# Turning the probability-times-value product of one attention block around: values as the stationary operand

## The chip, the cores and the metric

The kernel runs on one core of a Trainium2 chip. The metric is the time of one execution in microseconds (us) of device time. Of the core's engines, PE (TensorE) multiplies matrices (its loads of stationary operands are listed apart, as PEld), DVE (VectorE) and ACT (ScalarE) do elementwise work and read what PE leaves in PSUM, POOL (GpSimd) does elementwise work in SBUF alone, and SP (SyncE) issues most DMA transfers.

## What is computed

Two transformer blocks over 256 tokens of width 1024, all in 32-bit floating point. The first has sixteen attention heads of width 64 (eight "fox" heads with a forget gate, eight "moba" heads with a relative bias), then a mixture of 32 experts; the second has a Fourier branch, a differential attention and two dense feed-forward layers. Only the attention of the first block is touched. For each head, cut from the reference:

```
s = einsum('bhqd,bhkd->bhqk', q, k) * scale      # plus gate or bias terms, causal mask
p = softmax(s, axis=-1)
y = einsum('bhqk,bhkd->bhqd', p, v)
...
mix = concatenate([y_a, y_b], axis=-1)           # 16 heads x 64 = 1024 features
x = x + gt_m * rms_norm(mix @ w_out, g_post_mix)
```

## The kernel before

Queries are cut into two tiles of 128. The causal mask leaves the first tile 128 keys and the second 256, so the probabilities of a head are one tile `s` of 128 x 384. A head h goes through these helpers:

- `scores(h)`: PE writes q k^T into a PSUM tile of the name `sc` (two buffers, shared with several other steps).
- `soft(h)`: for each query tile DVE adds bias and mask and finds the largest score (L671), ACT takes the exponential and its row sums (L673); at the end DVE inverts both sums (L675, tile `sm`). `s` stays undivided.
- `trans(h)`: three PE transposes of `s` into the PSUM tile `pt` (L684); ACT (odd heads, and all from 8 on) or DVE copies it to the SBUF tile `st`.
- `pv(h)`: three matmuls (L701, L702, L704) with a 128 x 128 piece of `st` as the stationary operand and 64 columns of v as the moving one. Queries come out on partitions, a pair of heads beside each other in the one PSUM tile `mix`. DVE then multiplies each query tile by its inverse sum into an SBUF tile `mix` (L707).
- `mixT(j)`: two PE transposes of head pair j (L713) put features on partitions, in a tile `sc`; ACT rounds it to the high part `mh` (L714), DVE subtracts for the low part `ml` (L715; both are `big_h` and `big_l` in the trace). They are the stationary operands of the output projection.

The order of all engines' work is the order in which the code is written: step by step over h, and every engine takes its instructions in that order. Steps 0 to 7 (fox) are mixed with projections for the moba heads. In steps 8 to 16 the helper `out_products(n)` puts n units of the output projection (three matmuls of 512 columns each) between `scores` and `pv`, and `Stream` splits the next weight piece into high part (ACT, L250) and low part (DVE, L251). Steps 8 to 11 also hold a long DVE reduction for the modulation vector, `ada_cols` (L375). The core of a step from 8 on:

```
trans(h - 1); scores(h); soft(h)
...
out_products({8: 2, 9: 2, 11: 2, 13: 2, 16: 2}.get(h, 4))
j = {9: 3, 11: 4, 13: 5, 15: 6}.get(h)
if j:
    mixT(j)
...
pv(h - 1)
```

Pairs 0 and 1 are turned in step 7, pair 2 in step 8, pair 7 after the last step. Behind the attention stand the residual, the second norm, the router and the experts, whose weights come through a ring of 2 MB buffers; further buffers of it open when the attention's are given back.

Of the kernel before, what the change touches and what calls it, by code (L numbers as in the profile page):

```python
# [21 lines left out]
F32 = mybir.dt.float32  # L22
# [4 lines left out]
AF = mybir.ActivationFunctionType  # L27
OP = mybir.AluOpType
# [4 lines left out]
T, D, KD = 256, 1024, 8  # L33
# [62 lines left out]
def build(tc, A, out, dbg=None):  # L96
    nc = tc.nc
# [28 lines left out]
    ident, ones, iota, sel3 = c1[:, 0:128], c1[:, 128:256], c1[:, 256:384], c1[:, 384:416]  # L126
# [513 lines left out]
    PT = {}  # L640

    def head(h):
        return ("a", h) if h < 8 else ("b", h - 8)
# [19 lines left out]
    def soft(h):  # L663
        p = PT[h]
        n, hd = head(h)
        s = pa.tile([128, 384], F32, name="s", bufs=2)
        nm = pa.tile([128, 2], F32, name="nm", bufs=2)
        sm = pa.tile([128, 2], F32, name="sm", bufs=4)
        b = mask if n == "a" else biasM[:, hd]
        for i, (c0, c1_, b0) in enumerate(((0, 128, 128), (128, 384, 0))):  # L670
            nc.vector.tensor_tensor_reduce(out=s[:, c0:c1_], in0=p[:, i, 0:c1_ - c0], in1=b[:, b0:256], scale=-1.0,  # L671
                                           scalar=3.0e38, op0=OP.add, op1=OP.min, accum_out=nm[:, i:i + 1])
            nc.scalar.activation(s[:, c0:c1_], s[:, c0:c1_], AF.Exp, bias=nm[:, i:i + 1], scale=-1.0,  # L673
                                 accum_out=sm[:, i:i + 1])
        nc.vector.reciprocal(sm, sm)  # L675
        PT[h] = (s, sm)

    pmix, st_ = {}, {}

    def trans(h):  # L680
        s, _ = PT[h]
        pt = ps.tile([128, 384], F32, name="pt", bufs=1)
        for i in range(3):
            nc.tensor.transpose(pt[:, 128 * i:128 * i + 128], s[:, 128 * i:128 * i + 128], ident)  # L684
        st_[h] = pa.tile([128, 384], F32, name="st", bufs=2)
        if h % 2 or h > 7:
            nc.scalar.activation(st_[h], pt, AF.Copy)
        else:
            nc.vector.tensor_copy(st_[h], pt)

    def pv(h):
        n, hd = head(h)
        _, sm = PT.pop(h)
        st = st_.pop(h)
        if h % 2 == 0:
            pmix[h // 2] = (ps.tile([128, 2, 128], F32, name="mix", bufs=1),
                            pa.tile([128, 2, 128], F32, name="mix", bufs=4))
        pm_, mx = pmix[h // 2]
        o = slice(64 * (h % 2), 64 * (h % 2) + 64)
        v = vt[n][:, :, 64 * hd:64 * hd + 64]  # L700
        nc.tensor.matmul(pm_[:, 0, o], lhsT=st[:, 0:128], rhs=v[:, 0], start=True, stop=True, skip_group_check=True)  # L701
        nc.tensor.matmul(pm_[:, 1, o], lhsT=st[:, 128:256], rhs=v[:, 0], start=True, stop=False,  # L702
                         skip_group_check=True)
        nc.tensor.matmul(pm_[:, 1, o], lhsT=st[:, 256:384], rhs=v[:, 1], start=False, stop=True,  # L704
                         skip_group_check=True)
        for i in range(2):
            nc.vector.tensor_scalar(mx[:, i, o], pm_[:, i, o], sm[:, i:i + 1], None, op0=OP.mult)  # L707

    def mixT(j, tag="sc", bufs=2):
        _, mx = pmix.pop(j)  # L710
        pt = ps.tile([128, T], F32, name=tag, bufs=bufs)
        for i in range(2):
            nc.tensor.transpose(pt[:, 128 * i:128 * i + 128], mx[:, i], ident)  # L713
        nc.scalar.activation(mh[:, j], pt, AF.Copy)  # L714
        nc.vector.tensor_tensor(ml[:, j], pt, mh[:, j].bitcast(F32), op=OP.subtract)  # L715


    proj_out("b")
    for h in range(8):
# [5 lines left out]
        if h > 1:  # L725
            soft(h)
# [4 lines left out]
        j = {1: 4, 3: 5, 4: 6, 6: 7}.get(h)  # L731
# [96 lines left out]
    for h in range(8, 17):  # L828
# [11 lines left out]
        j = {9: 3, 11: 4, 13: 5, 15: 6}.get(h)  # L840
# [15 lines left out]
        if h == 14:  # L856

            lgc = pa.tile([128, NE], F32, name="lgc")
            p = ps.tile([128, NE], F32, name="sc", bufs=2)
            for k in range(KD):  # L860
                nc.tensor.matmul(p, lhsT=mod[:, 24 + k:25 + k].to_broadcast([128, 128]), rhs=wr[:, k], start=(k == 0),
                                 stop=(k == KD - 1))
            nc.vector.tensor_add(lgc, p, V("b_router"))
        if h == 15:
# [196 lines left out]
    for i in range(4):  # L1061
        nc.tensor.matmul(pm[:, i], lhsT=rows[i // 2][:, 128 * (i % 2):128 * (i % 2) + 128], rhs=sel4[:, 0:2], start=True,
                         stop=True, skip_group_check=True)

    p = ps.tile([128, 4, 128], F32, name="pt", bufs=1)
    for tt in range(2):
        for k in range(KD):
            nc.tensor.matmul(p[:, k % 4, 64 * (k // 4):64 * (k // 4) + 64], lhsT=h2t[:, tt, 128 * k:128 * k + 128],
                             rhs=S0[:, tt], start=(tt + k == 0), stop=(tt == 1), skip_group_check=True)
# [12 lines left out]
    ps = fm.enter_context(tc.tile_pool(name="pse", bufs=1, space=PSUM, reuse_waits="tile"))  # L1082
# [359 lines left out]
    for e in range(NE):  # L1442
# [5 lines left out]
        if e == NE - 1:  # L1448
# [7 lines left out]
        v = nc.values_load(cnt[0:1, e:e + 1], engines=[ET.PE, ET.Activation, ET.DVE], min_val=0, max_val=T,  # L1456
                           skip_runtime_bounds_check_because="a count of at most 256 tokens")
# [77 lines left out]
    for k in range(KD):  # L1535
        nc.tensor.matmul(acc[k], lhsT=pend[0][:, 128 * k:128 * k + 128], rhs=pend[1], start=False, stop=True,
                         skip_group_check=True)
# [516 lines left out]
```

## Time and profile before

| what | value |
|---|---|
| time, median of 3 runs | 1770.94 us (1769.97 to 1772.21) |
| time of the profiled execution | 1769.94 us |
| span in its trace | 1768.1 us |
| PE busy | 1501.6 us, 85% of the span |
| PE weight loads | 984.5 us, 56% |
| DVE busy | 779.3 us, 44% |
| ACT busy | 522.3 us, 30% |
| mean granted TensorE clock | 0.949 of full |
| read from HBM | 545.25 MB, 309 GB/s over the span |

The attention of the first block lies between 75 and 190 us of the span; the experts between 214 and 1265 us; the second block fills the rest. Shares over the whole span mix these stages, so they say nothing on the change by themselves. The time is 1.8 us more than the span.

### The profile page before, as it was taken

How to read it: one execution, taken by the hardware profiler on the slowest of the kernel's cores; microseconds unless marked ns; L12 is line 12 of the kernel's file. 1: busy time of each engine (PE TensorE's matmuls, PEld its weight loads, DVE VectorE, ACT ScalarE, POOL GpSimd, SP SyncE). 2: the span in 40 equal slices, each digit the busy share in tenths (PEclk: the TensorE clock that was granted, in tenths of full speed). 3: DMA queues.
4: the chain of work that ended last, by engine and by line, in shares of the span. 5: the costliest groups of instructions: out<-in, count | busy, mean ns of one | idle time of the engine just before them, and what ended most of it. 6: DMA issues, size and time to landing. Idle time of an engine off the chain costs nothing. (4 is left out here: it accounts for less than half of the span.)

```text
span 1768.1 us, 26974 instructions
## 1 busy us (share of the span) xinstructions
PE 1501.6 (85%) x10842; PEld 984.5 (56%) x10842; DVE 779.3 (44%) x1605; ACT 522.3 (30%) x1114; POOL 106.5 (6%) x114
## 2 busy tenths in 40 slices
PE   6999978967779888778868776668999999999998
PEld 5787623323233332332323222227999989999997
DVE  5776613233332432433211111115766767676665
ACT  4544311101011010110101101005544556565444
POOL 3501100000000000000000000002000100310000
PEclk8999999998999999999979888889999999999999
DMA  9878779999999979999999999995554553344630
GB/s 353 323 229 340 277 271 414 417 415 416 416 401 412 413 290 366 415 415 417 406 383 402 409 416 416 416 414 218 191 205 159 193 201 144 143 165 170 221 137 25
DMA packets 89049, 549.49 MB, mean 311 GB/s; under 512 B 5064, under 2 KB 7912, under 8 KB 49448
## 3 DMA queue, kind: packets, MB, share of 16 engines
q1 hardware_dynamic: 88424, 544.55, 77.9%
q8 instruction: 154, 2.52, 0.6%
q0 software_dynamic: 272, 0.92, 0.2%
q10 hardware_dynamic: 144, 1.05, 0.2%
q14 instruction: 55, 0.45, 0.1%
HBM read 545.25 MB, written 1.25 MB: 309 GB/s over the span
## 5 line engine op out<-in xcount | busy, mean ns | idle before, releaser
L251 DVE TENSOR_TENSOR wl<-ring,wh 128x512 fp32r<-128x512 f32 x421 | 284.9, 710 | 114.8 <-ACT wh L250 108.1
L250 ACT ACTIVATE wh<-ring 128x512 fp32r<-128x512 f32 x424 | 248.7, 622 | 106.5 <-PE gu L281 86.1
L1259 PE MATMUL h<-ring,xe 128*32 128x512 f32 x1280 | 194.5, 733 | 56.4 <-DMA ring<-in_w_gate_up 32.4
L280 PE MATMUL gu<-ring,wh 128*128 128x256 f32 x704 | 201.2, 286 | 2.9 <-ACT ring L1586 2.9
L281 PE MATMUL gu<-ring,wh 128*128 128x256 f32 x704 | 200.4, 285 | 1.9 <-DVE ring L1590 1.9
L282 PE MATMUL gu<-ring,wl 128*128 128x256 f32 x704 | 200.4, 285 | 0.0
L1155 PE MATMUL h<-ring,xe 128*64 128x512 f32 x768 | 173.6, 594 | 11.4 <-DMA ring<-in_w_gate_up 9.8
L1259 PEld LDWEIGHTS h<-ring,xe 128*32 128x32 f32 x1280 | 50.4, 127 | 181.5 <-issue 145.8
L1264 DVE TENSOR_SCALAR glu<-h 64x512 f32<-64x512 f32 x23 | 15.7, 683 | 287.5 <-PE h L1259 287.5
L280 PEld LDWEIGHTS gu<-ring,wh 128*128 128x128 f32 x704 | 135.9, 193 | 3.5 <-ACT ring L1586 3.3
L281 PEld LDWEIGHTS gu<-ring,wh 128*128 128x128 f32 x704 | 135.9, 193 | 2.2 <-DVE ring L1590 2.1
L282 PEld LDWEIGHTS gu<-ring,wl 128*128 128x128 f32 x704 | 135.9, 193 | 0.0
L1117 ACT ACTIVATE xg<-rot 128x512 f32<-128x512 f32 x28 | 16.7, 597 | 381.4 <-PE rot L1114 381.4
L1155 PEld LDWEIGHTS h<-ring,xe 128*64 128x64 f32 x768 | 56.6, 137 | 113.1 <-issue 96.5
L280 PE MATMUL pd<-acth,wh 128*128 128x256 f32 x352 | 98.8, 281 | 0.1
L281 PE MATMUL pd<-actl,wh 128*128 128x256 f32 x352 | 98.3, 279 | 0.1
L282 PE MATMUL pd<-acth,wl 128*128 128x256 f32 x352 | 98.2, 279 | 0.0
L1286 PE MATMUL h<-ring,aT 128*32 128x256 f32 x1280 | 78.2, 394 | 21.2 <-ACT aT L1281 10.7
L1195 PE MATMUL h<-ring,aT 128*64 128x512 f32 x384 | 86.7, 605 | 6.4 <-ACT aT L1175 6.4
L1372 DVE COPY_PREDICATED bias<-bm,vecs 128x512 f32<-128x512 uint8 x124 | 80.0, 726 | 1.1
L1160 DVE TENSOR_SCALAR glu<-h 128x512 f32<-128x512 f32 x12 | 8.3, 692 | 160.6 <-PE h L1155 160.6
L280 PE MATMUL gu<-big_h,wh 128*128 128x256 f32 x256 | 74.6, 291 | 0.0
(446 smaller groups left out, 2450.2 us busy)
## 6 DMA issues: line engine op xcount, KB each, us to landing
ring<-in_w_gate_up SPq DMA_DIRECT2D x127, 2048.0 KB, 23.2
ring<-in_w_down SPq DMA_DIRECT2D x62, 2048.0 KB, 24.6
ring<-in_ffn_gu SPq DMA_DIRECT2D x22, 2048.0 KB, 8.0
ring<-in_win SPq DMA_DIRECT2D x12, 2048.0 KB, 8.2
ring<-in_ffn_wd SPq DMA_DIRECT2D x10, 2048.0 KB, 9.5
ring<-in_ada SPq DMA_DIRECT2D x8, 2048.0 KB, 11.5
ring<-in_wout SPq DMA_DIRECT2D x4, 2048.0 KB, 7.8
ring<-in_ada SPq DMA_DIRECT2D x4, 1024.0 KB, 12.4
```

The source lines that it names most:

```text
L250: nc.scalar.activation(dh, src, AF.Copy)
L251: (eng or nc.vector).tensor_tensor(dl, src, dh.bitcast(F32), op=OP.subtract)
L280: nc.tensor.matmul(o, lhsT=wh, rhs=mh, start=start, stop=False, skip_group_check=True)
L281: nc.tensor.matmul(o, lhsT=wh, rhs=ml, start=False, stop=False, skip_group_check=True)
L282: nc.tensor.matmul(o, lhsT=wl, rhs=mh, start=False, stop=stop, skip_group_check=True)
L1117: nc.scalar.activation(x, p, AF.Copy)
L1155: nc.tensor.matmul(p[64 * hf:64 * hf + 64], lhsT=x, rhs=wk[:, 512 * hf:512 * hf + 512], start=False, stop=(k == KD - 1), skip_group_check= ...
L1195: nc.tensor.matmul(py[64 * oh_:64 * oh_ + 64], lhsT=at[:, j, 64 * c:64 * c + 64], rhs=wk[:, 512 * oh_:512 * oh_ + 512], start=False, stop= ...
L1259: nc.tensor.matmul(p[32 * g:32 * g + 32], lhsT=x(k), rhs=w[:, k % 2, c], start=False, stop=(k == KD - 1), skip_group_check=True)
L1264: nc.vector.tensor_scalar(g, p[0:64], 7.0, None, op0=OP.min)
L1286: nc.tensor.matmul(py[32 * g:32 * g + 32, 0:T], lhsT=at[:, j, 32 * c:32 * c + 32], rhs=w[:, j, T * g:T * g + T], start=False, stop=(c == 1 ...
L1372: nc.vector.copy_predicated(bias2[:, h], m, val[:, :, None].to_broadcast([128, 2, T]))
```

## The change

`soft` divides: after L675, DVE multiplies both pieces of `s` by the inverse sums (new L677, 128 x 128 and 128 x 256). `pv` becomes two matmuls (new L702, L703) with 64 columns of v as the stationary operand and `st` as the moving one (256 and 128 columns), so a head's features come out on 64 partitions of a PSUM tile `mix` of 128 x 256 and a pair fills it. L707's multiplications go, and so do `mixT`'s transposes: ACT (new L711) and DVE (new L712) read the pair as it is. For pairs 0 to 2 DVE first copies it to SBUF (new L707); from pair 3 on they read the PSUM tile itself. That tile has one buffer.

```diff
         nc.vector.reciprocal(sm, sm)
-        PT[h] = (s, sm)
+        for i, c in enumerate((slice(0, 128), slice(128, 384))):
+            nc.vector.tensor_scalar(s[:, c], s[:, c], sm[:, i:i + 1], None, op0=OP.mult)
+        PT[h] = s
...
     def pv(h):
...
         if h % 2 == 0:
-            pmix[h // 2] = (ps.tile([128, 2, 128], F32, name="mix", bufs=1),
-                            pa.tile([128, 2, 128], F32, name="mix", bufs=4))
-        pm_, mx = pmix[h // 2]
+            pmix[h // 2] = ps.tile([128, T], F32, name="mix", bufs=1)
+        p = pmix[h // 2]
...
-        nc.tensor.matmul(pm_[:, 0, o], lhsT=st[:, 0:128], rhs=v[:, 0], start=True, stop=True, skip_group_check=True)
-        nc.tensor.matmul(pm_[:, 1, o], lhsT=st[:, 128:256], rhs=v[:, 0], start=True, stop=False,
+        nc.tensor.matmul(p[o], lhsT=v[:, 0], rhs=st[:, 0:256], start=True, stop=False, skip_group_check=True)
+        nc.tensor.matmul(p[o, 128:256], lhsT=v[:, 1], rhs=st[:, 256:384], start=False, stop=True,
                          skip_group_check=True)
-        nc.tensor.matmul(pm_[:, 1, o], lhsT=st[:, 256:384], rhs=v[:, 1], start=False, stop=True,
-                         skip_group_check=True)
-        for i in range(2):
-            nc.vector.tensor_scalar(mx[:, i, o], pm_[:, i, o], sm[:, i:i + 1], None, op0=OP.mult)
-
-    def mixT(j, tag="sc", bufs=2):
-        _, mx = pmix.pop(j)
-        pt = ps.tile([128, T], F32, name=tag, bufs=bufs)
-        for i in range(2):
-            nc.tensor.transpose(pt[:, 128 * i:128 * i + 128], mx[:, i], ident)
-        nc.scalar.activation(mh[:, j], pt, AF.Copy)
-        nc.vector.tensor_tensor(ml[:, j], pt, mh[:, j].bitcast(F32), op=OP.subtract)
+        if h in (1, 3, 5):
+            pmix[h // 2] = pa.tile([128, 256], F32, name="mix", bufs=4)
+            nc.vector.tensor_copy(pmix[h // 2], p)
+
+    def mixT(j):
+        p = pmix.pop(j)
+        nc.scalar.activation(mh[:, j], p, AF.Copy)
+        nc.vector.tensor_tensor(ml[:, j], p, mh[:, j].bitcast(F32), op=OP.subtract)
```

Three places in the order of instructions show what moves. On PE in step 9, with the semaphores that an instruction waits for in brackets, this is the piece from `mixT(3)` over `pv(8)` to `trans(9)` (`vb` is v of the moba heads, `c_70` the identity):

```order
-L713 MATMUL sc<-c_70,mix 128x128 [waits DVE_49] x2
-L701 MATMUL mix<-vb,st 128x64 [waits Activation_49]
-L702 MATMUL mix<-vb,st 128x64
-L704 MATMUL mix<-vb,st 128x64
-L684 MATMUL pt<-c_70,s 128x128 [waits PE_49,Activation_49]
-L684 MATMUL pt<-c_70,s 128x128 [waits Activation_49]
-L684 MATMUL pt<-c_70,s 128x128
-L659 MATMUL sc<-qkb 128x128 [waits DVE_49]
+L702 MATMUL mix<-st,vb 64x256 [waits DVE_49]
+L703 MATMUL mix<-st,vb 64x128
+L686 MATMUL pt<-c_70,s 128x128 [waits PE_49]
+L686 MATMUL pt<-c_70,s 128x128 x2
```

The first matmul of `pv(8)` waited for ACT (the copy `st`) and now waits for a count of DVE's; the wait of the next scores (L659) for DVE is gone.

On DVE in the same step, from the inverse sums of head 9 on, this stood there before (`ring` holds the modulation weights and the weight piece):

```order
L675 RECIPROCAL sm<-sm 128x2 [waits Activation_49]
L375 ISA ring_1076,mod<-ring_1076,csb 128x1024
L375 ISA mod 128x1
L251 TENSOR_TENSOR wl<-ring_941,wh 128x512 [waits Activation_49]
L715 TENSOR_TENSOR big_l<-sc,big_h 128x256 [waits Activation_49]
```

This stands there now:

```order
L675 RECIPROCAL sm<-sm 128x2 [waits Activation_49]
L677 TENSOR_SCALAR s<-s,sm 128x128 [waits DVE_49]
L677 TENSOR_SCALAR s<-s,sm 128x256
L375 ISA ring_1079,mod<-ring_1079,csb 128x1024
L375 ISA mod 128x1
L251 TENSOR_TENSOR wl<-ring_941,wh 128x512 [waits Activation_49]
L712 TENSOR_TENSOR big_l<-mix,big_h 128x256 [waits Activation_49]
```

L712 stands where L715 stood, behind the same reduction and split and two scalings more; it now reads the PSUM tile `mix` that `pv(8)` writes next.

On DVE in step 1, behind the sums of head 0, the scalings come ahead of two weight splits and the copy of the transposed head:

```order
-L251 TENSOR_TENSOR wl<-ring_284,wh 128x512 [waits DVE_49,Activation_49] x2
-L689 COPY st<-pt 128x384 [waits PE_49]
+L677 TENSOR_SCALAR s<-s,sm 128x128 [waits DVE_49]
+L677 TENSOR_SCALAR s<-s,sm 128x256
+L251 TENSOR_TENSOR wl<-ring_284,wh 128x512 [waits Activation_49] x2
+L691 COPY st<-pt 128x384 [waits PE_49]
```

The transposes of head 0 (L686) now follow these scalings, where they followed ACT's exponentials.

## Rows read from the trace of the kernel before

**Rows 1.** Stretches: busy us of PE, PEld, DVE, ACT, POOL; granted clock, DMA share, GB/s.

```profile
175.00:186.00 11.00, 11.00 (x79) 8.83 (x79) 4.93 (x16) 4.22 (x11) 0.00 (x0) 1.00 0.31 102
200.00:214.00 14.00, 13.10 (x98) 11.50 (x100) 7.96 (x38) 4.36 (x11) 1.03 (x2) 0.88 0.95 376
214.00:1265.00 1051.00, 816.78 (x5594) 350.71 (x5591) 308.32 (x640) 150.24 (x332) 25.30 (x26) 0.92 0.95 383
```

**Rows 2.** Timeline of step 9, DVE and PE: start, us, operation, idle before.

```profile
148.29 0.17 DVE L675 RECIPROCAL sm<-sm 128x2 f32<-128x2 f32 x1 [0.77 <-ACT s L673]
148.38 1.20 DVE L375 CUSTOM_DVE_ANT_0 ring<-ring,csb 128x1024 f32<-128x1024 f32 x1
149.51 0.69 DVE L251 TENSOR_TENSOR wl<-ring,wh 128x512 fp32r<-128x512 f32 x1
150.11 0.41 DVE L715 TENSOR_TENSOR big_l<-sc,big_h 128x256 fp32r<-128x256 f32 x1
...
148.27 0.38 PE L713 MATMUL sc<-c,mix 128*128 128x128 f32 x2
148.49 0.33 PE L701 MATMUL mix<-vb,st 128*128 128x64 f32 x2
...
149.11 0.49 PE L684 MATMUL pt<-c,s 128*128 128x128 f32 x3
```

**Rows 3.** Timeline of DVE in the second block's attention, which scales such a tile.

```profile
1426.91 0.17 DVE L1754 RECIPROCAL sm<-sm 128x2 f32<-128x2 f32 x1 [0.82 <-ACT s L1752]
1427.11 0.16 DVE L1755 TENSOR_TENSOR sm<-sm,nlam 128x1 f32<-128x1 f32 x1
1427.19 0.35 DVE L1756 TENSOR_SCALAR s<-s,sm 128x256 f32<-128x256 f32 x1
```

**Rows 4.** Timeline of DVE and PE around steps 7 to 9.

```profile
140.09 0.17 DVE L675 RECIPROCAL sm<-sm 128x2 f32<-128x2 f32 x1 [0.71 <-ACT s L673]
141.89 0.29 DVE L671 CUSTOM_DVE_ANT_0 s<-sc,bias 128x128 f32<-128x128 f32 x1 [0.40 <-issue]
146.88 0.29 DVE L671 CUSTOM_DVE_ANT_0 s<-sc,bias 128x128 f32<-128x128 f32 x1 [0.42 <-PE sc L659]
...
144.78 0.43 PE L701 MATMUL mix<-va,st 128*128 128x64 f32 x2
```

**Rows 5.** Timeline of steps 13 and 14, DVE and PE.

```profile
166.64 0.17 DVE L675 RECIPROCAL sm<-sm 128x2 f32<-128x2 f32 x1 [0.77 <-ACT s L673]
166.83 0.33 PE L701 MATMUL mix<-vb,st 128*128 128x64 f32 x2
169.24 0.92 PE L659 MATMUL sc<-qkb 64*128 64x128 f32 x4 [0.36 <-ACT csb L810]
```

**Rows 6.** Timeline of step 15, DVE and PE.

```profile
179.04 0.17 DVE L675 RECIPROCAL sm<-sm 128x2 f32<-128x2 f32 x1 [0.77 <-ACT s L673]
180.62 0.33 PE L701 MATMUL mix<-vb,st 128*128 128x64 f32 x2
```

**Rows 7.** Timeline of step 1, DVE and PE.

```profile
86.15 0.17 DVE L675 RECIPROCAL sm<-sm 128x2 f32<-128x2 f32 x1 [0.71 <-ACT s L673]
86.17 0.44 PE L684 MATMUL pt<-c,s 128*128 128x128 f32 x2 [0.17 <-ACT s L673]
```

**Rows 8.** Timeline of PE's weight loads behind the last head pair's transposes.

```profile
186.78 0.19 PEld L280 LDWEIGHTS mm<-wh,big_h 128*128 128x128 f32 x1 [0.21 <-ACT big_h L714]
```

**Rows 9.** Timeline of PE in the second block: two f32 products of 256 moving columns.

```profile
1455.83 1.02 PE L1778 MATMUL ot<-atT,ring 128*128 128x256 f32 x4
1456.78 0.70 PE L1746 MATMUL sc<-ring 64*128 64x256 f32 x4
```

**Rows 10.** Stretches among the experts, as in Rows 1, around idle times of PE.

```profile
448.80:455.00 6.20, 3.27 (x24) 0.90 (x24) 0.28 (x2) 0.00 (x0) 0.00 (x0) 1.00 1.01 418
512.00:515.10 3.10, 0.02 (x3) 0.00 (x0) 2.82 (x5) 0.63 (x1) 0.00 (x0) 0.96 1.01 414
515.10:521.70 6.60, 5.55 (x28) 2.88 (x32) 6.49 (x13) 0.77 (x2) 0.00 (x0) 0.50 0.99 395
```

More of the change, by code (lines that the diff above doesn't have):

```diff
@@ L675, in soft @@
         nc.vector.reciprocal(sm, sm)
-        PT[h] = (s, sm)
+        for i, c in enumerate((slice(0, 128), slice(128, 384))):
+            nc.vector.tensor_scalar(s[:, c], s[:, c], sm[:, i:i + 1], None, op0=OP.mult)
+        PT[h] = s
     pmix, st_ = {}, {}
     def trans(h):
-        s, _ = PT[h]
+        s = PT.pop(h)
         pt = ps.tile([128, 384], F32, name="pt", bufs=1)
@@ L692, in pv @@
         n, hd = head(h)
-        _, sm = PT.pop(h)
         st = st_.pop(h)
         if h % 2 == 0:
-            pmix[h // 2] = (ps.tile([128, 2, 128], F32, name="mix", bufs=1),
-                            pa.tile([128, 2, 128], F32, name="mix", bufs=4))
-        pm_, mx = pmix[h // 2]
+            pmix[h // 2] = ps.tile([128, T], F32, name="mix", bufs=1)
+        p = pmix[h // 2]
         o = slice(64 * (h % 2), 64 * (h % 2) + 64)
         v = vt[n][:, :, 64 * hd:64 * hd + 64]
-        nc.tensor.matmul(pm_[:, 0, o], lhsT=st[:, 0:128], rhs=v[:, 0], start=True, stop=True, skip_group_check=True)
-        nc.tensor.matmul(pm_[:, 1, o], lhsT=st[:, 128:256], rhs=v[:, 0], start=True, stop=False,
+        nc.tensor.matmul(p[o], lhsT=v[:, 0], rhs=st[:, 0:256], start=True, stop=False, skip_group_check=True)
+        nc.tensor.matmul(p[o, 128:256], lhsT=v[:, 1], rhs=st[:, 256:384], start=False, stop=True,
                          skip_group_check=True)
-        nc.tensor.matmul(pm_[:, 1, o], lhsT=st[:, 256:384], rhs=v[:, 1], start=False, stop=True,
-                         skip_group_check=True)
-        for i in range(2):
-            nc.vector.tensor_scalar(mx[:, i, o], pm_[:, i, o], sm[:, i:i + 1], None, op0=OP.mult)
-    def mixT(j, tag="sc", bufs=2):
-        _, mx = pmix.pop(j)
-        pt = ps.tile([128, T], F32, name=tag, bufs=bufs)
-        for i in range(2):
-            nc.tensor.transpose(pt[:, 128 * i:128 * i + 128], mx[:, i], ident)
-        nc.scalar.activation(mh[:, j], pt, AF.Copy)
-        nc.vector.tensor_tensor(ml[:, j], pt, mh[:, j].bitcast(F32), op=OP.subtract)
+        if h in (1, 3, 5):
[5 more added lines that the diff above has]
+        nc.vector.tensor_tensor(ml[:, j], p, mh[:, j].bitcast(F32), op=OP.subtract)
     proj_out("b")
```

## The prediction

> **What bounds the kernel now.** The change sits in one stage, so I read the stretches by stage first. At the end of the attention PE is busy in all 11.00 us of 175 to 186, with the DMA engines at 0.31 of their time [rows 1]: PE sets the pace, the ring of weight buffers is full, and a transfer has to wait for a buffer. The experts behind it run with DMA at 0.95 over 1051 us [rows 1]; they consume a stream that starts anew when the attention's buffers are given back. So a microsecond won or lost by PE before 190 us should reach the end of the kernel one for one: nothing behind it waits for something that started earlier. Then I read the timeline of single steps, PE and DVE beside each other, since the change hands work from PE to DVE and gives PE new waits.
>
> In step 9 the reader is to see two chains that did not touch. DVE takes the inverse sums at 148.29, then the long reduction L375, the split L251, and only at 150.11 the subtraction L715 of head pair 3, which ends at 150.52. PE meanwhile has turned that pair (L713 at 148.27) into its own `sc` buffer and starts `pv(8)` at 148.49 [rows 2]. It could, because `mix` in PSUM had been emptied by L707 a step earlier.
>
> **The change part by part.**
>
> *The scalings on DVE.* A dependent operation starts 0.20 after a reciprocal [rows 3]; an independent one starts 0.09 after it [rows 2]. The piece of 256 columns takes 0.35 [rows 3]. The piece of 128 columns is not in the trace; it lies between the 0.17 of a two-column reciprocal and that 0.35, and I take 0.28. Each operation starts 0.08 before its forerunner's end (148.38 against 148.46 [rows 2]). So everything behind L675 moves by 0.11 + 0.20 + 0.27 = 0.58 us, sixteen times. Most of this is covered: a head's transposes come one step later, behind projection matmuls. L707's two multiplications, which go, had cost DVE about as much; the three new copies are covered too, the pair being needed steps later. The exception is step 1, where the transposes of head 0 waited for ACT until 86.17 [rows 7]. The last two will wait for the second scaling: 86.15 + 0.20 + 0.20 + 0.35 + 0.03 for the signal (1427.08 to 1427.11 [rows 3]) = 86.93. **+0.8 us.**
>
> *The transposes of pairs.* Two of them hold PE for 148.49 - 148.27 = 0.22 us [rows 2]; with them go the visits of `mixT` to the two `sc` buffers.
>
> *The new wait.* From pair 3 on, ACT's L711 and DVE's L712 read the single PSUM tile `mix`, and `pv` of the next even head, which overwrites it, stands right behind in the code. PE takes its matmuls in order, so `pv`, the transposes and the next scores all queue behind L712, and L712 queues on DVE behind the scalings, the reduction and the split of the same step.
>
> - Steps 7 to 9. DVE's inverse sums at 140.09 will be followed by the scalings (0.67 until the next may start) and two L712 (0.33 each, 0.41 less the overlap); so head 8's softmax starts at about 141.4 where it was 141.89 [rows 4]. On PE six transposes vanish (3 x 0.22) and some waits for `sc` buffers; I estimate 1.0 us for both, by which `pv(7)`, at 144.78 before [rows 4], comes earlier. DVE gains as much: 141.4, 1.41 to the inverse sums of head 8 (as 146.88 to 148.29 for head 9), 0.67, L712 0.33, reduction and split 1.73 (148.38 to 150.11), and an addition of L715's size 0.33 make 145.9 for the softmax of head 9; its scores on PE allow 146.0, against 146.88 [rows 4]. From there: 1.41 to the inverse sums, 0.58 more than before for the scalings, 2.23 to the end of the subtraction (148.29 to 150.52), 0.03 of signal: `pv(8)` starts at 150.25, not 148.49: **+1.8 us**. PE, ready at about 147.3, idles for 3.0 us.
> - Step 11 repeats step 9 within 0.01 us, without a gain ahead: `pv(10)` starts 0.20 after the inverse sums before, and now 0.58 + 2.23 + 0.03 = 2.84 after: **+2.6 us**, and 2.9 idle (it is ready 0.22 earlier, the transposes being gone).
> - Step 13 has no reduction. 166.64 + 0.67 + 0.60 for the split (149.51 to 150.11) + 0.41 + 0.03 = 168.35 against 166.83. As `mixT(5)` takes no `sc` buffer any more, the 0.36 that the next scores waited for goes [rows 5]: **+1.2 us**.
> - Step 15 has two splits: 179.04 + 0.67 + 1.20 + 0.44 = 181.35 against 180.62 [rows 6]: **+0.7 us**.
> - The last pair has no `pv` behind it. It saves its transposes and the 0.21 of wait for L714 [rows 8]: **-0.45 us**.
>
> *The matmuls of `pv`.* Before, 0.62 us a head (148.49 to 149.11 [rows 2]). After, 384 moving columns. The lower bound is no change. The nearest row is a pair of f32 products with 256 moving columns each, 0.95 us from start to start [rows 9]; 384/512 of it is 0.71. The scores, which move the same 128 and 256 columns, give the upper bound: 0.92 [rows 5]. I take 0.71, the stationary shape being nearest: 16 x 0.09 = **+1.4 us**, with 0 to +4.8 as bounds. [...]
>
> *The clock.* PE has not been idle in this stage and its granted clock is 1.00 [rows 1]. Two idle times of about 3 us are new. [...] I take one fall for the two pauses: **+1.7 us**. [...]
>
> **The sum.** 0.8 + 1.8 + 2.6 + 1.2 + 0.7 - 0.45 = 6.65 of waits, 1.4 of matmuls, 1.7 of clock: 9.75 us. On the profiled execution's 1769.94 us (a span of 1768.1 and 1.8 around it) that is 1779.7 us. This execution lies 1.0 under the median of the three runs.
>
> **The rivals.**
>
> 1. *No fall of the clock.* Dense 512-column matmuls stand on both sides of each pause, denser than around the pauses among the experts. Then 1769.94 + 8.05 = 1778.0 us.
> 2. *Both pauses are paid.* [...] 1779.7 + 1.7 = 1781.4 us.
> 3. *Not slower: `pv` does not wait.* The mechanism is the place of L712. It decides whether L711 and L712 have ended when PE finishes the units ahead of `pv`: for that L712 would have to end 3.0, 2.9, 1.7 and 1.0 us sooner than above, as it would if DVE had it ahead of the reduction and the split. Then only the savings are left: +0.8 - 1.0 - 4 x 0.22 - 0.36 - 0.45 + 1.4 = -0.5, so 1769.4 us. Against it: the order on DVE, and the bracket on `pv(8)`'s first matmul.
> 4. *The delay is taken up later.* If the expert stage were held by a transfer that starts at a time of its own, these 10 us would vanish into it, and the time be about 1771 us. Against it: DMA at 0.31 just before the hand-over [rows 1].
>
> **How the numbers follow.** The forecast of one fall gets 0.40, no fall 0.27, two falls 0.15, no wait 0.08, taken up later 0.05, and 0.05 goes to costs I do not see, mostly slower. A measurement of this kernel can tell about 0.2%, 3.5 us, from no change. All the waiting cases lie over that: 0.86 for slower. The no-wait case and the swallowed delay lie within: 0.11; 0.03 is left for faster. The three waiting cases span 1778.0 to 1781.4. The bounds of `pv`'s price would put them between 1776.6 and 1784.8; the waits are worked out to perhaps 2 us, mostly the start of head 9's softmax. I take 1774.5 to 1783.5.
>
> **What would show it.** In the trace after: four idle times of PE ahead of L702 of heads 8, 10, 12 and 14, released by DVE's L712, near 3.0, 2.9, 1.7 and 1.0 us, and none as long elsewhere in the stage; `pv(7)` about a microsecond earlier relative to head 7's scores; L677 at about 0.28 and 0.35 us; a granted clock under 1.00 in one stretch between 150 and 175; the start of the experts later by the same sum. I am wrong if PE starts L702 of head 8 with no idle time before it, if a head's two matmuls take well over 0.71 us, or if the experts start late but the end does not move.

## The result, and the profile after

The changed kernel takes 1790.91 us (median of six runs, 1783.29 to 1792.59) against 1770.51 for the kernel before on the same chip: 20.4 us more by the medians, or 1.15%; the ratio worked out over all runs is 1.0105 (95% interval 1.0091 to 1.012). It is slower, as forecast, but by twice the 9.75 us of the sum, and outside the range. The profiled execution took 1791.03 us, with a span of 1789.2. PE is busy 85% of the span as before, so the whole-span shares again show nothing.

The stage does. Stretches of the kernel after, columns as in [rows 1]:

```profile
85.00:95.00 10.00, 9.07 (x43) 5.37 (x44) 6.31 (x16) 4.37 (x11) 2.12 (x2) 0.83 0.69 233
145.00:155.00 10.00, 8.39 (x42) 4.80 (x42) 7.01 (x23) 4.55 (x15) 1.34 (x2) 0.83 0.99 422
155.00:165.00 10.00, 7.67 (x22) 5.22 (x23) 5.11 (x15) 2.82 (x8) 0.00 (x0) 0.66 0.94 388
165.00:175.00 10.00, 7.31 (x46) 4.43 (x45) 4.74 (x14) 2.76 (x8) 0.00 (x0) 0.97 0.15 32
175.00:186.00 11.00, 10.32 (x35) 7.08 (x34) 4.62 (x21) 4.40 (x13) 2.72 (x8) 0.72 0.85 355
```

The same stretches of the kernel before:

```profile
85.00:95.00 10.00, 9.83 (x56) 6.83 (x55) 7.22 (x20) 6.41 (x17) 1.57 (x2) 1.00 0.78 295
145.00:155.00 10.00, 10.00 (x68) 7.34 (x68) 8.10 (x27) 4.82 (x14) 0.00 (x0) 1.00 1.00 417
155.00:165.00 10.00, 10.00 (x59) 7.81 (x58) 6.67 (x26) 5.30 (x15) 0.84 (x3) 1.00 0.97 371
165.00:175.00 10.00, 9.64 (x62) 8.15 (x61) 4.79 (x18) 5.10 (x15) 1.87 (x6) 1.00 0.65 270
```

Two columns tell it: PE has holes (7.67 and 7.31 of 10 us where it had 10.00 and 9.64), and its granted clock, 1.00 throughout before, is lower in all five stretches, most in four of them. Between 160 and 163 us it is 0.50. At a mean of 0.66, the 7.67 busy us of 155 to 165 are worth some 5 at the full clock (an estimate, the product of the two).

The holes are the announced ones. Step 9 of the kernel after, the timeline of DVE, then of ACT and PE, beside [rows 2]:

```profile
154.44 0.17 DVE L675 RECIPROCAL sm<-sm 128x2 f32<-128x2 f32 x1 [0.71 <-ACT s L673]
154.64 0.55 DVE L677 TENSOR_SCALAR s<-s,sm 128x128 f32<-128x128 f32 x2
155.10 1.22 DVE L375 CUSTOM_DVE_ANT_0 ring<-ring,csb 128x1024 f32<-128x1024 f32 x1
...
156.25 0.69 DVE L251 TENSOR_TENSOR wl<-ring,wh 128x512 fp32r<-128x512 f32 x1
156.85 0.42 DVE L712 TENSOR_TENSOR big_l<-mix,big_h 128x256 fp32r<-128x256 f32 x1
...
154.83 0.36 ACT L711 ACTIVATE big_h<-mix 128x256 fp32r<-128x256 f32 x1
...
154.24 0.39 PE L282 MATMUL vv<-wh,big_l 128*128 128x512 f32 x1
157.33 1.11 PE L702 MATMUL mix<-st,vb 128*64 128x256 f32 x2 [2.70 <-DVE big_l L712]
158.23 0.63 PE L703 MATMUL mix<-st,vb 128*64 128x128 f32 x2
158.80 0.90 PE L686 MATMUL pt<-c,s 128*128 128x128 f32 x3
161.21 0.79 PE L280 MATMUL mm<-wh,big_h 128*128 128x512 f32 x1
161.80 0.63 PE L281 MATMUL mm<-wl,big_h 128*128 128x512 f32 x1
```

ACT is done with the pair at 155.19; DVE gets to the subtraction only at 156.85, behind the scalings, the reduction and the split, and PE starts 0.06 us after it ends. The four idle times of PE ahead of L702 are 2.70, 2.69, 1.57 and 0.77 us (3.0, 2.9, 1.7 and 1.0 were forecast). The expectations below count the same waits by the idle time of the weight loads: 3.12, 3.12, 2.00 and 1.19. Then the second loss shows: the two matmuls behind the hole take 1.47 us up to the transposes (158.80 - 157.33), where head 0's two take 0.79 (97.76 to 98.55). The granted clock is 0.51 over those 1.47 us, and 1.00 at head 0's (97.7 to 98.6 us).

The waits of the kernel after, between 85 and 200 us (who waits for whom: us in all, times, longest):

```profile
PE mix L702 <- DVE big_l L712: 7.0, 3, 2.7
...
PE pt L686 <- DVE s L677: 2.2, 3, 0.9
```

The first line holds three of the four idle times, the last lying behind 200 us. The second, 0.93 us in step 1 and 0.39 and 0.90 in step 8, was in the forecast for step 1 alone.

### The profile page after: what moved, and what is told of

It reads as the page before. It is cut to its first block, busy times and chain, and to the rows that moved or that the text cites. A ratio compares the mean times of both kernels' runs of the same rounds, so it can differ in the third digit from the quotient of the medians.

```text
span 1789.2 us, 26835 instructions
## 1 busy us (share of the span) xinstructions
PE 1515.9 (85%) x10794; PEld 987.1 (55%) x10794; DVE 782.9 (44%) x1608; ACT 522.5 (29%) x1114; POOL 106.6 (6%) x114
## 5 line engine op out<-in xcount | busy, mean ns | idle before, releaser
L1256 PE MATMUL h<-ring,xe 128*32 128x512 f32 x1280 | 196.7, 727 | 75.6 <-issue 52.2
L1152 PE MATMUL h<-ring,xe 128*64 128x512 f32 x768 | 174.4, 598 | 7.9 <-DMA ring<-in_w_gate_up 6.4
L1256 PEld LDWEIGHTS h<-ring,xe 128*32 128x32 f32 x1280 | 52.1, 126 | 199.3 <-issue 173.0
L1261 DVE TENSOR_SCALAR glu<-h 64x512 f32<-64x512 f32 x23 | 15.7, 683 | 298.7 <-PE h L1256 298.7
L1152 PEld LDWEIGHTS h<-ring,xe 128*64 128x64 f32 x768 | 56.7, 137 | 110.5 <-issue 98.5
```

The source lines that it names most:

```text
L1152: nc.tensor.matmul(p[64 * hf:64 * hf + 64], lhsT=x, rhs=wk[:, 512 * hf:512 * hf + 512], start=False, stop=(k == KD - 1), skip_group_check= ...
L1256: nc.tensor.matmul(p[32 * g:32 * g + 32], lhsT=x(k), rhs=w[:, k % 2, c], start=False, stop=(k == KD - 1), skip_group_check=True)
L1261: nc.vector.tensor_scalar(g, p[0:64], 7.0, None, op0=OP.min)
```

## Experiments

Three theories, formed on that trace. Theory 1: the loss is made of the waits behind L712 (some 7 us), of clock falls behind PE's pauses (some 10), and of dearer products (some 2.7). Theory 2: the new form of the product itself costs most. Theory 3: the scalings cost most.

For every run the table gives how much later than in the profiled execution before PE starts the transposes of head 1, 6, ... 15: the difference of two start times of PE's matmuls from the timelines, so that one can see in which step time is lost. The first column is the scores of head 0, ahead of any change; it shows how far executions differ by themselves. The last two are the start of the last output product and the time, with its ratio to the kernel before beside it.

| us later than before | head 0 | 1 | 6 | 8 | 9 | 11 | 13 | 15 | last product | time, ratio [95%] |
|---|---|---|---|---|---|---|---|---|---|---|
| before, start | 75.8 | 95.4 | 136.6 | 145.5 | 149.1 | 158.7 | 168.4 | 182.3 | 189.4 | 1770.3 to 1770.9 |
| changed | 0.5 | 3.2 | 4.6 | 6.2 | 9.7 | 15.2 | 20.3 | 21.0 | 20.9 | 1790.91, 1.0105 [1.0091, 1.012] |
| changed, again | 0.7 | 1.8 | 3.2 | 5.1 | 8.7 | 15.9 | 20.1 | 20.8 | 20.8 | 1788.44, 1.0100 [1.0084, 1.0116] |
| scalings alone | 0.2 | 2.6 | 4.1 | 7.1 | 7.1 | 7.1 | 7.1 | 7.1 | 7.1 | 1780.18, 1.0062 [1.0040, 1.0084] |
| product form alone | -0.3 | 0.0 | 1.5 | 1.5 | 1.9 | 2.3 | 3.0 | 3.5 | 3.7 | not comparable |
| copies | -1.9 | 2.2 | 3.6 | 5.3 | 5.4 | 5.6 | 6.0 | 5.8 | 5.8 | 1779.49, 1.0053 [1.0036, 1.0070] |
| mixT first | -0.2 | 2.5 | 3.9 | 4.1 | 4.2 | 4.5 | 5.0 | 4.8 | 4.8 | 1776.95, 1.0031 [1.0020, 1.0042] |
| four pauses filled | 0.2 | 2.9 | 4.3 | 5.8 | 8.7 | 11.8 | 13.8 | 14.5 | 14.5 | 1790.16, 1.0105 [1.0079, 1.0130] |
| the same, again | 0.2 | 1.3 | 2.7 | 4.3 | 7.3 | 10.4 | 12.4 | 13.0 | 13.0 | 1790.39, 1.0112 [1.0093, 1.0130] |
| all pauses filled | 0.1 | 2.3 | 3.8 | 4.7 | 7.7 | 10.8 | 12.8 | 13.5 | 13.5 | 1787.18, 1.0093 [1.0074, 1.0113] |
| no masks | 0.4 | 3.0 | 4.5 | 3.4 | 6.3 | 9.7 | 14.4 | 15.1 | 15.1 | 1787.42, one run |
| all moved | 0.1 | -0.1 | 1.4 | 2.4 | 5.0 | 5.3 | 5.7 | 5.6 | 5.6 | 1775.04, 1.0024 [1.0013, 1.0035] |
| all moved, masks spread | -0.5 | -0.7 | 0.7 | 0.8 | 0.9 | 1.3 | 1.7 | 1.6 | 1.6 | 1774.68, 1.0014 [1.0004, 1.0024] |
| delay at the end | -0.4 | -0.4 | -0.4 | -0.4 | -0.4 | -0.3 | -0.3 | -0.3 | 14.5 | 1784.46, 1.0078 [1.0065, 1.0091] |

### The two parts apart

The scalings alone, on the kernel before:

```diff
         nc.vector.reciprocal(sm, sm)
+        for i, c in enumerate((slice(0, 128), slice(128, 384))):
+            nc.vector.tensor_scalar(s[:, c], s[:, c], sm[:, i:i + 1], None, op0=OP.mult)
...
-            nc.vector.tensor_scalar(mx[:, i, o], pm_[:, i, o], sm[:, i:i + 1], None, op0=OP.mult)
+            nc.vector.tensor_copy(mx[:, i, o], pm_[:, i, o])
```

> The kernel before, with one part of the change alone: each head's probabilities are divided ahead of their transposes, and the two multiplications after the products become copies of the same size. The products and mixT stay as before. Theory 1: VectorE is later by two scalings a head; TensorE waits for them 1 us or less in steps 1, 7 and 8, with a fall of the clock behind the one in step 1 or behind that in step 7 as in the changed kernel: 1771 to 1776 us. Theory 2 (the product form costs most): 1770 to 1773 us. Theory 3 (the scalings cost most, with GpSimd's mask additions beside them in step 7): 1780 us or more.

The product form alone, on the kernel before:

```diff
+        nc.tensor.matmul(p[o], lhsT=v[:, 0], rhs=st[:, 0:256], start=True, stop=False, skip_group_check=True)
+        nc.tensor.matmul(p[o, 128:256], lhsT=v[:, 1], rhs=st[:, 256:384], start=False, stop=True,
...
+        if h % 2:
+            for i in range(2):
+                nc.vector.tensor_scalar(mx[:, i], p[:, 128 * i:128 * i + 128], sm[:, i:i + 1], None, op0=OP.mult)
```

> The kernel before, with the other part alone: v is the stationary, so that a head takes two matmuls (64 columns held; 256 and 128 passed) in place of three; the product is scaled once a pair of heads by two multiplications of 128 columns in place of two of 64 a head, and mixT transposes as before. Probabilities are not divided ahead of their transposes, and the scaling takes the odd head's sums, along the wrong axis: this part of the computation is changed. Theory 1: 16 heads at 0.17 us more a head by the products' rows of the changed kernel, of which part hides; no long wait; 1771 to 1775 us. Theory 2 (the product form itself costs most of the 20 us): 1780 us or more. Theory 3: 1770 to 1773 us.

In the stage the form costs 3.7 us, nearly evenly over the heads, and the scalings 7.1, all of it up to head 8. From head 8 to head 15, where the changed kernel loses 14.8, the scalings alone lose nothing and the form alone 1.9. Both runs still copy the pair to SBUF and transpose it: that L711 and L712 read the PSUM tile itself, the third part of the change, is in neither, and the next two runs take it up. Theory 2 falls. Theory 3 had 1780 us or more for the scalings and is right on that (1780.18); theory 1 gave them too little (1771 to 1776). But they are about a third of the loss at most. Up to head 8 the two parts add up to 8.6 us, where the changed kernel is at 6.2, and 1.5 of the 7.1 are a fall of the clock that no long pause explains: over 125 to 145 us it is at 0.91, with PE busy 25.00 of the 25 us ahead and 19.17 of those 20 (19.26 in the kernel before, at 1.00), and the 1.5 us are lost by the transposes of head 6 at 140.7. Theory 1 has no place for such a fall. The final time of the form alone (1759.6 us) says nothing: its values change the routing, and the experts' product L1154 runs 832 times in it where its counterpart runs 768 times in the kernel after.

### The waits taken away

Two ways. Copies: the pair is copied out of the PSUM tile for all pairs but the last.

```diff
-        if h in (1, 3, 5):
+        if h in (1, 3, 5, 7, 9, 11, 13):
```

> The changed kernel, with the pair of heads copied by VectorE out of the shared PSUM tile after heads 7, 9, 11 and 13 too, as it is already after 1, 3 and 5; mixT then reads the copy. Theory 1 (the 20.4 us over before are the waits of the first product of heads 8, 10, 12 and 14 for mixT's subtraction, some 7 us, the clock falls that follow pauses, some 10 us of lost speed, and dearer products, some 2.7 us): the idle time before those products (3.12, 3.12, 2.00 and 1.19 us) goes, and with it the falls of the granted clock near 157 and 174 us, while the falls near 89 and 147 us stay; 1775 to 1778 us. Theory 2 (the new product form itself, 64 columns held and 256 passed, costs most): the copies take away the waits alone, 1783 us or more. Theory 3 (the scalings ahead of the transposes cost most, by their own waits in steps 1, 7 and 8): 1784 us or more.

mixT first: L711 and L712 stand ahead of the step's softmax.

```diff
         if h > 8:
             trans(h - 1)
+        j = {9: 3, 11: 4, 13: 5, 15: 6}.get(h)
+        if j:
+            mixT(j)
         if h < 16:
             scores(h)
             soft(h)
```

> The changed kernel, with mixT of the pairs 3, 4, 5 and 6 issued ahead of the scores and the softmax in steps 9, 11, 13 and 15, so that VectorE's queue has the subtraction ahead of the reduction, the scalings and the split. No copy is added. Theory 1 (queue order on VectorE makes the first product of heads 8, 10, 12 and 14 wait): the four waits (3.12, 3.12, 2.00, 1.19 us) fall below 0.5 us each, the falls of the clock near 157 and 174 us go, and the stage ends some 5 to 6 us later than before's, as in the run with copies: 1775 to 1780 us. If the wait were for ScalarE's copy of the pair or for the shared tile in another way: the waits stay above 1.5 us each and the time above 1784 us.

PE's weight loads for the first product of heads 8, 10, 12 and 14 with mixT first, and for one head between:

```profile
152.47 0.19 PEld L702 LDWEIGHTS mix<-st,vb 128*64 128x64 f32 x2 [0.36 <-issue]
...
162.34 0.19 PEld L702 LDWEIGHTS mix<-st,vb 128*64 128x64 f32 x2 [0.36 <-issue]
167.88 0.19 PEld L702 LDWEIGHTS mix<-st,vb 128*64 128x64 f32 x2
171.59 0.19 PEld L702 LDWEIGHTS mix<-st,vb 128*64 128x64 f32 x2 [0.36 <-issue]
...
185.36 0.19 PEld L702 LDWEIGHTS mix<-st,vb 128*64 128x64 f32 x2 [0.35 <-DVE s L677]
```

No wait is left: in either run PE itself is idle for less than 0.3 us ahead of each of these products. From head 8 to head 15 only 0.8 us is lost (0.6 with the copies), where the changed kernel lost 14.8. Some 14 us of the stage's 21, waits and clock falls together, thus come from one fact: `pv` waits for L712, which stands far back in DVE's queue. Freeing the tile sooner by a copy and moving L712 ahead both undo it. By their times, mixT first (1776.95) lies in theory 1's range and the copies (1779.49) 1.5 us over theirs; both are below the others'.

### The pauses filled

The waits stay, but PE does useless work in them: 24, 24, 13 and 7 matmuls in steps 9, 11, 13 and 15, ahead of the waiting products of heads 8, 10, 12 and 14 (the expectation names the steps as heads).

```diff
+        n_fill = {9: 24, 11: 24, 13: 13, 15: 7}.get(h, 0)
+        if n_fill:
+            idle = ps.tile([128, 384], F32, name="pt", bufs=1)
+            for _ in range(n_fill):
+                nc.tensor.matmul(idle[:, 0:256], lhsT=mh[:, 0, 0:128], rhs=mh[:, 0], start=True, stop=True,
+                                 skip_group_check=True)
         pv(h - 1)
```

> The changed kernel, with 24, 24, 13 and 7 matmuls that compute nothing needed (128 columns held, 256 passed, into the PSUM tile of the transposes) ahead of the first product of heads 9, 11, 13 and 15, in the place where TensorE's queue would otherwise come to the waiting products. Theory 1 (waits some 7 us and clock falls some 10 us): the waiting products start no earlier, or a little later, but TensorE is busy meanwhile, and the granted clock does not fall near 157 and 174 us: 1783 to 1786 us, faster than the changed kernel by 5 to 8 us although it does more. If the clock plays no part, and only the waits count: 1790 to 1793 us, no faster than the changed kernel. Theory 2 (the product form costs most): 1790 to 1793 us too.

Timeline of PE in step 9 with the pauses filled, and under it two stretches:

```profile
153.84 0.39 PE L282 MATMUL vv<-wh,big_l 128*128 128x512 f32 x1
154.07 3.03 PE L848 MATMUL pt<-big_h 128*128 128x256 f32 x24
157.03 0.65 PE L702 MATMUL mix<-st,vb 128*64 128x256 f32 x2
...
157.82 0.55 PE L686 MATMUL pt<-c,s 128*128 128x128 f32 x3
...
155.00:165.00 10.00, 10.00 (x68) 7.07 (x66) 5.91 (x16) 2.99 (x8) 0.00 (x0) 1.00 0.88 357
175.00:186.00 11.00, 11.00 (x62) 8.42 (x62) 4.61 (x22) 5.24 (x15) 2.72 (x8) 1.00 0.53 222
```

The product starts 2.96 us behind the first useless matmul, about as long a wait as before; but the granted clock stays at 1.00, the two matmuls take 0.79 again, and the stage ends 6.4 us sooner (14.5 against 20.9) with 68 matmuls more. From head 8 to head 15, around the filled pauses, it loses 8.7 us in place of 14.8: the 6.1 between them are the clock by itself. The kernel's time did not follow: at 1790.16 us it is where the rival without the clock had it (1790 to 1793), not at theory 1's 1783 to 1786. So both were run again, without an edit:

> The kernel with the four idle times filled, once more, for more executions and a second profile: its stage ended 14.5 us later than before's, 6.5 ahead of the changed kernel's, but the kernel's median was 1790.2 us. If the excess behind the stage is chance of single executions: the stage again ends 14 to 15 us later, and the median lies near 1785 us. If the stage's gain is truly given back behind it: 1789 to 1791 us again.

> The changed kernel itself once more, beside the run with the idle times filled, on the same chip: does the stage again end 21 us later than before's, with falls at the same places (theory 1: yes, within 1 us), and what does the rest add? 1789 to 1792 us.

Stretches of the changed kernel in this second profile:

```profile
85.00:95.00 10.00, 9.05 (x49) 6.18 (x50) 7.19 (x20) 5.35 (x16) 2.26 (x2) 1.00 0.75 249
...
155.00:165.00 10.00, 8.71 (x22) 5.99 (x23) 4.94 (x15) 2.63 (x7) 0.00 (x0) 0.53 0.86 354
...
175.00:186.00 11.00, 10.20 (x40) 6.97 (x38) 4.78 (x21) 4.90 (x14) 2.71 (x8) 0.80 0.85 358
```

The stage repeats: 13.0 against 20.8, and from head 8 to head 15 8.7 against 15.7, a difference of 7.0. So does the end: 1790.39 and 1788.44. The gain is lost among the experts. Their first product (L1152 in the kernel after) starts 6.5 and 7.7 us sooner in the filled versions (228.1 against 234.6, 227.9 against 235.6); at some 885 us they are still 5.6 to 5.9 ahead (the last L1256 on `xq` starts at 883.2 and 884.7 against 889.1 and 890.3); the last start of L1152, near 980 us, is only 0.5 and 1.2 ahead (979.0 against 979.5, 979.8 against 981.0). The stretch from 250 to 1230 us of the changed kernel, and of the one with four pauses filled:

```profile
250.00:1230.00 980.00, 750.17 (x5108) 294.00 (x5108) 265.81 (x555) 118.07 (x271) 19.93 (x20) 0.92 0.98 398
```

```profile
250.00:1230.00 980.00, 749.14 (x5092) 294.88 (x5092) 265.02 (x555) 116.10 (x267) 20.26 (x21) 0.91 0.98 395
```

There the weights arrive at 395 GB/s in place of 398 (each in both profiles), and DMA is at 0.98. Three of 398 over 980 us is an estimate of 7.4 us, the size of what is missing. Why the transfers are slower there, whether by their phase or by the clock of 0.91, these runs don't settle; mixT first, which fills no pause, has 396 GB/s at 0.91.

Filling the two places where PE waits for scalings as well, with ten f32 matmuls (`fill_f32` is a loop like the one above over columns of k):

```diff
+        if h == 1:
+            fill_f32(kT["a"], 5)
         if h >= 1:
             trans(h - 1)
...
             mixT(2)
+            fill_f32(kT["b"], 5)
             trans(h - 1)
```

> The kernel with the idle times filled (68 useless matmuls ahead of the first products of heads 9, 11, 13 and 15), and ten more (f32, 128 columns held, 256 passed) in the two places where TensorE waits for scalings: five ahead of the transposes of head 0 and five ahead of those of head 7. Theory 1 (behind each idle time the granted clock falls, and a fall costs 1.5 to 3 us of TensorE's work): no fall is left between 80 and 200 us, the two near 89 and 147 us too are gone, and the stage ends 10.5 to 12.5 us later than before's, where it ended 14.5 later with the four idle times filled and 21 later with none; the time 1781 to 1786 us. If the falls near 89 and 147 us do not come from the idle times there: they stay, and the stage ends 14 us later than before's or more.

No fall is left in the stage (a clock of 1.00 over 85 to 200 us), as expected of theory 1, but it ends at 13.5, not by 12.5, and the time of 1787.18 us is over the 1786 expected: head 1 is 2.2 us behind head 0 instead of the 1.1 that the wait alone costs, so the useless matmuls were longer than the wait they fill.

### GpSimd beside the scalings

In steps 6 and 7 GpSimd adds the causal mask to the bias of the second set of heads (L517), in four instructions. Timelines of the kernel after in steps 7 and 8: DVE, POOL, PE's weight loads of head 7's transposes.

```profile
144.91 1.58 DVE L677 TENSOR_SCALAR s<-s,sm 128x128 f32<-128x128 f32 x2
...
141.40 4.93 POOL L517 TENSOR_TENSOR bias<-bias,c 128x512 f32<-128x512 f32 x4 [51.91 <-PE mm L282]
...
146.54 0.20 PEld L686 LDWEIGHTS pt<-c,s 128*128 128x128 f32 x2 [1.09 <-DVE s L677]
```

The pair takes 1.58 us, 0.55 elsewhere, and ends 0.16 us behind GpSimd's last mask addition. The run without those additions:

```diff
-        if h >= 6:
-            moba_mask(2 * h - 12)
-            moba_mask(2 * h - 11)
```

> The changed kernel without GpSimd's four mask additions on the second set of heads: their causal mask, a part of the computation, is left out. For the scalings of head 7, whose 256-column half took 1365 ns beside those additions, against 319 to 348 elsewhere. If a scaling waits while GpSimd has an addition under way: that pair takes 0.55 us in place of 1.58, the transposes of head 7 wait 0.1 us or less in place of 1.09, and TensorE is 1 us ahead of the changed kernel at the end of step 8. If the long scaling has another cause (the sums, VectorE's queue): it stays above 1.2 us. No final time is expected: without the masks the probabilities differ.

Its timeline of DVE, and a stretch:

```profile
144.77 0.55 DVE L677 TENSOR_SCALAR s<-s,sm 128x128 f32<-128x128 f32 x2
...
145.00:155.00 10.00, 7.10 (x44) 4.44 (x45) 8.06 (x27) 4.60 (x15) 0.00 (x0) 1.00 0.99 420
```

The pair is back at 0.55, the clock fall of that stretch is gone (1.00 where it was 0.83), and head 8 is at 3.4 where it was at 6.2: PE is 2.7 us ahead of the changed kernel, where 1 was expected. PE's wait for the scalings ahead of head 7's transposes is 0.38 us in place of 0.39 and 0.90, not the 0.1 expected. Beside the additions the 256-column scaling took 1365 ns in place of some 350, and the pair ended 0.16 us behind the last addition; an addition takes 1261 ns in the mean. That the scaling waits for an addition under way is the author's estimate from these times; how the one holds up the other was not shown.

A second trait of this run: it has two pauses alike, PE's 2.70 us in step 9 and 2.69 in step 11 (up to 154.6 and 167.15 us). The stretches behind them:

```profile
155.00:165.00 10.00, 9.46 (x56) 5.91 (x54) 5.39 (x20) 4.77 (x14) 0.00 (x0) 1.00 0.91 375
165.00:175.00 10.00, 7.85 (x22) 5.44 (x23) 4.57 (x14) 2.64 (x8) 0.00 (x0) 0.66 0.77 294
```

The clock stayed at 1.00 after the first and fell after the second. The length of a pause alone does not decide it.

### What a delay there is worth, and all the moves

116 useless matmuls ahead of the last output products of the kernel before:

```diff
+        if h == 16:
+            idle = ps.tile([128, 384], F32, name="pt", bufs=1)
+            for _ in range(116):
+                nc.tensor.matmul(idle[:, 0:256], lhsT=mh[:, 0, 0:128], rhs=mh[:, 0], start=True, stop=True,
```

> The kernel before with 116 matmuls that compute nothing needed (128 columns held, 256 passed) ahead of the last output products: a delay at the end of the attention stage by 116 x 0.126 us (24 such took 3.03 us in the run with the idle times filled) = 14.6 us, with TensorE busy throughout. It asks what a delay at that place is worth at the end of the kernel, since in the run with the idle times filled the stage ended 14.5 us later than before's and the kernel 19. Handed on one to one: 1784 to 1786 us. Taken up in part by the weights' transfers behind it: 1780 us or less. Made larger by what follows: 1788 us or more.

The stage ends 14.5 us later, the kernel 13.5 (1784.46 - 1770.94): handed on nearly one to one.

All waits moved behind other work: mixT first, and three moves more.

```diff
-        if h >= 1:
+        if h > 1:
             trans(h - 1)
+        if h == 7:
...
+            mixT(0)
+            mixT(1)
         scores(h)
...
+                if k == 5:
+                    trans(0)
                 if k == 4 * h + 2:
...
-        j = {9: 3, 11: 4, 13: 5, 15: 6}.get(h)
+        j = {8: 2, 9: 3, 11: 4, 13: 5, 15: 6}.get(h)
...
         out_products({8: 2, 9: 2, 11: 2, 13: 2, 16: 2}.get(h, 4))
+        if h == 8:
+            trans(h - 1)
```

> As the run before it, and three moves more: the transposes of head 0 stand in the middle of v's projection in step 1, mixT of the pairs 0 to 2 stands ahead of the scores in steps 7 and 8, and the transposes of head 7 stand behind the first output products in step 8. Theory 1 (what is left of the loss is TensorE's waits for the scalings in steps 1, 7 and 8, each with a clock fall behind it, some 2.9 and 2 us in the run of the scalings alone): the attention stage ends 1 to 3 us later than before's, and the time is 1769 to 1775 us. Theory 2 (the form costs most by itself): the stage ends 5 us later or more, 1775 us or more.

Step 1 then costs nothing, but the stage ends where theory 2 had it (5 us or more): 2.6 us are lost behind step 8, with the clock at 0.68 from 143 to 153 us: beside the mask additions two subtractions of DVE now took 2.35 us (0.74 elsewhere) and a pair of scalings 1.26 (0.55). So the masks were spread, the product form staying as it is:

```diff
-        if h >= 6:
-            moba_mask(2 * h - 12)
-            moba_mask(2 * h - 11)
+        if h == 7:
+            moba_mask(0)
...
+        if h in (8, 10, 12):
+            moba_mask(h // 2 - 3)
```

> The version with all moves, and GpSimd's mask additions spread: one in step 7 and one each behind steps 8, 10 and 12, in place of four at once beside the work of steps 7 and 8, where in that version two subtractions of 256 columns took 2.35 us and a pair of scalings 1.26. Theory 1 (VectorE waits there for GpSimd, TensorE for VectorE, and the clock falls behind it): no fall of the clock is left in the stage, which ends 2 to 3.5 us later than before's in place of 5.8, and the time is 1769 to 1774 us, the same as before within what can be told. If GpSimd has nothing to do with it: the stage ends 5 us later or more. What is left is the price of the products, which this version does not change, so no gain over before is expected.

Timeline of DVE and stretches in that run:

```profile
138.25 2.75 DVE L712 TENSOR_TENSOR big_l<-mix,big_h 128x256 fp32r<-128x256 f32 x2
...
142.47 0.55 DVE L677 TENSOR_SCALAR s<-s,sm 128x128 f32<-128x128 f32 x2
...
145.00:155.00 10.00, 9.47 (x52) 6.25 (x56) 8.25 (x27) 5.27 (x16) 0.00 (x0) 1.00 0.57 241
155.00:165.00 10.00, 10.00 (x57) 6.74 (x47) 7.47 (x26) 4.80 (x14) 0.00 (x0) 1.00 0.00 0
```

Three of the four additions still ran together, from 138 us on, but now beside two subtractions that had time to spare. The stage ends 1.6 us later than before's, 2.1 from head 0 on, with the clock at 1.00, so the 5.6 was not the form's. The kernel is at 1774.68 us, 0.7 over the 1774 expected and a ratio of 1.0014 to before; its median is 3.9 us over before's, 2.3 more than the stage explains, and these runs don't tell why. No version beat the kernel before. What remains in the stage is, by this account, mostly the price of the product form, which no run here takes away.

## Why the prediction was wrong

The direction, the mechanism and its place were right; the size was not, and mainly by one step.

- **The clock: the step that failed.** "I take one fall for the two pauses: +1.7 us." No run shows that term. Both long pauses were paid, and the clock cost 6.1 us in one pair of executions and 7.0 in the other (changed against filled, from head 8 to head 15). Four pauses were filled, but behind the third the changed and the filled kernel both lose 0.7 us (head 13 to head 15), so the cost lies behind the two long ones. The forecast also read PE as never idle in this stage; before has idle times of up to 0.46 us between 86 and 186, with no fall behind them (1.00 over 85 to 200). The term was mis-sized twice. It counted one fall where there were two (of the two idle times in [rows 10] one has 0.50 behind it, the other 1.00), and its 1.7 us are 14.00 x (1 - 0.88), from a stretch among other work [rows 1]: by the same sum, 155 to 165 at 0.66 gives 3.4 us, twice the 1.7 (an estimate). Pauses of 1 us or so, which the forecast did not count, were paid as well, though not always. In step 1 the changed kernel lost 2.7 us in one execution, with the clock at 0.83 in the stretch from 85 us, and 1.1 in the second (1.8 - 0.7), where that stretch is at 1.00; in six of the eight profiles with this pause of 0.9 us the clock fell behind it. Rival 2, both pauses paid, was right in kind; its two falls, 3.4 us, were half of what the rows show. Not every long pause is paid, though: that in step 9 of the run without masks was not. All this is measured in the stage; at the end of the kernel the runs with filled pauses gave the gain back, and what the clock costs there stays open.
- **Steps 7 to 9: right without the masks.** +1.8 us was worked out from head 6 to the transposes of head 9. The run without masks has 6.3 - 4.5 = 1.8. The changed kernel has 9.7 - 4.6 = 5.1: the forecast gave L677 0.28 and 0.35 us, which is what the pairs take, but did not look at what GpSimd does beside one of them. `pv(7)`, forecast a microsecond earlier against head 7's scores, came 1.5 us later (150.86 - 141.90 in place of 144.78 - 137.28); without the masks it came 1.1 earlier (148.13 - 141.76). This was left out altogether, and is the second error: 3.3 us, of which an estimate of 1.7 is a fall again (0.83 from 145 to 155).
- **The other waits: right.** PE's four idle times are within 0.3 us of the forecast, and a little shorter. Steps 10 and 11, with the pauses filled so that the clock stays out: 11.8 - 8.7 = 3.1 us, of which the products of two heads are some 0.3 to 0.6; 2.6 was forecast. Steps 12 and 13: 2.0, against 1.2 and products. Steps 14 and 15: 0.7 with products, against 0.7 without. Step 1: 1.1 without a fall, 0.8 forecast.
- **The products: some three times the term.** 0.79 us a head against 0.71 taken, and 0.29 a head over before in heads 1 to 6 (4.6 - 3.2 over five heads): 0.17 in the two products, the rest in the matmuls beside them. The form alone cost 3.7 us in the stage, and 16 x 0.29 would be 4.6, where the sum has 1.4 (within its bounds of 0 to 4.8). It shows where no wait is left: rival 3's sum without the 0.8 of step 1 is -1.3, and the run with everything moved and the masks spread has 2.1.
- **Handed on: right.** The experts' first product starts 21.0 us later (234.6 against 213.6). A delay of 14.5 us at the end of the stage came out as 13.5 at the end of the kernel; the changed kernel's 20.9 as 20.4. The runs with filled pauses are the exception.

Added up at head 15: 0.5 of difference before head 0; 2.7 in step 1; 1.4 for the products up to head 6; 5.1 in steps 7 to 9; 5.5 in 10 and 11 and 5.1 in 12 and 13, of which the clock is 6.1 with its part in step 9; 0.7 after. That is 21.0. Theory 1 holds for the changed kernel with an addition, the masks, which belong to neither theory. Open are the slower transfers behind the runs with filled pauses, and the fall in the run of the scalings alone that has no long pause ahead of it.

## What to carry to other kernels

When a change makes PE read a result sooner or share a tile longer, look at what stands ahead of the releasing instruction in the other engine's queue: moving one subtraction a step, with ACT's copy beside it, ahead of the softmax took away two thirds of this loss. Price a pause of PE as pause plus lost clock, and count short pauses too: in this stage the clock added nearly as much (6.1 to 7.0 us) as the four waits (7.7). Before giving VectorE SBUF-to-SBUF work, look at the row of GpSimd beside it: the pair of scalings took 1.58 us beside its additions and 0.55 without them.

## What the runs showed of the hardware

- With PE kept busy by useless matmuls through two pauses of 2.7 us, no fall followed them in all three runs that did so (a granted clock of 1.00 from 155 to 186 us in one, 0.99 and 1.00 over 85 to 200 in the others); an idle pause of that length was followed by a fall in five of six cases: both in two executions of the changed kernel (0.66 from 155 to 165 and 0.72 from 175 to 186; 0.53 and 0.80), one of two without masks (1.00 from 155 to 165, 0.66 from 165 to 175). A pause of 0.9 us in step 1 was followed by one in six of eight profiles (from 85 to 95, 0.83 in the changed kernel's first execution, 1.00 in its second); a pause of 1.02 us in step 8 of the run with the masks spread was not (1.00 from 145 to 155).
- The clock also fell once with no long pause ahead of it: to 0.91 over 125 to 145 us in the run of the scalings alone, with PE busy 25.00 of the 25 us ahead and 19.17 of those 20, for 1.5 us of lost time.
- One VectorE scaling of 256 columns in SBUF took 1365 ns beside GpSimd's additions, where a pair of 128 and 256 columns takes 0.55 us elsewhere; a pair of subtractions took 2.75 us in place of 0.74. In the kernel before, a pair of subtractions that reads PSUM (L715 at 140.36) took 0.76 us beside the same additions.
- A head's two products in the new form take 0.79 us whether or not the scaling stands ahead of them, for 384 moving columns in f32: 2.06 ns a column, with 64 stationary columns.
